# Standing rounded weights placed 64 bytes into longer ring buffers

## The chip, the cores and the metric

The kernel runs on one core of one Trainium2 chip. The metric is the device time of one execution in microseconds. Before the change three runs gave 2685.96, 2694.65 and 2699.78 us; the median is 2694.65.

## The reference

Two layers of a decoder trunk over 256 tokens of width 2048, all in float32. Each layer mixes the tokens by two groups of heads (attention with a window of 128, and RWKV-7 with a delta rule) and then runs a SwiGLU network; both are modulated by a condition vector. Cut to what matters here:

```python
mod = (cond @ w_ada[l] + b_ada[l]).reshape(B, 6, 1, D)      # cond = silu(c); w_ada 2048 x 12288
u = x * (1 + sc_m) + sh_m
proj = u @ w_in[l]                                          # 2048 x 4896
y = concat(sliding_window_attention(proj[..., :1536]), rwkv7_group(proj[..., 1536:]))
x = layer_norm(alpha * x + gt_m * (y @ w_out[l]))           # 2048 x 2048
u = x * (1 + sc_f) + sh_f
gate, up = split(u @ w_gate_up[l])                          # 2048 x 11264
x = layer_norm(alpha * x + gt_f * ((silu(gate) * up) @ w_down[l]))   # 5632 x 2048
```

## The kernel before

Every large product is computed from rounded parts. A float32 operand is split into hi, its value rounded to the type float32r, and lo, the rounded rest; the product is the sum of three matmuls, hi by hi, hi by lo and lo by hi. The activations are split once and kept in left-hand tiles (`lhsp`, 17 buffers of 2,048 bytes per partition, each with both parts of 128 rows by 256 tokens). The weights are split as they come. The helper `steps` (line 376) allocates a `raw` buffer of 1,024 columns from a ring of four, has SyncE's queue fill it from HBM, and lets ScalarE write `hi` (line 392, ring of three) and VectorE write `lo` as raw minus hi (line 393, ring of two). It yields slices of both, and two kinds of loops consume them:

- `stream` (line 402): the activation stands in the array as `lhsT`, and the weight streams as `rhs`, mostly in pieces of 512 columns. Lines 414, 415 and 417 are its three matmuls. It serves the q, k, v projection, the output projection, and both products of the SwiGLU network. Where `room` is given, `hi` and `lo` are other tiles than the rings'.
- `tstream` (line 420): the weight stands in the array, 128 columns of it at a time (32 in one block), and the 256 tokens of an activation stream. The result comes out transposed, features on partitions. Lines 426, 427 and 428 are its three matmuls: hi by hi, hi by lo, lo by hi. It serves the part of the input projection that feeds RWKV-7: in `front` (line 475) the low-rank columns, the values and, for the first layer, some of r and k; in `project` (line 588) the rest of r and k.

Every matmul of the program is a weight load and a matmul on TensorE; the profile has them as PEld and PE.

The work around it is ordered by hand. Within the mixer a written-out list per layer (`ORDER`, line 41) sets when projections, chunks of the recurrence, attention heads and output products come; a planner orders the instructions of each engine when the program is built, by dependences. SyncE's queue carries all large transfers; w_ada comes through it too, in tiles `ast` that VectorE multiplies into `aacc` (line 264) beside the other work, and in the first layer ahead of the projection (lines 302 to 319). That first stretch lasts until about 160 us.

On-chip memory is laid out pool behind pool: `const`, then `lhsp` (17 x 2,048 bytes), `wp` (raw 4, hi 3 and lo 2, each of 4,096 bytes), `adap` (two `asum` buffers of 32 bytes, `aacc`, two `ast`, two `arow` of 512 bytes), and behind them pools that are opened and closed stage by stage. At the largest stage 320 bytes per partition remain free. The start of `lhsp`, `wp` and of each buffer in them is a multiple of 128 bytes, and the slices taken are multiples of 512, so all rounded operands of the three matmuls begin at multiples of 128. `crow` (line 160) is the condition's row of 16 partitions by 128, used once at the start; `arow` (line 296) is a small row tile with two buffers, used where the gates are written out.

Of the kernel before, what the change touches and what calls it, by code (L numbers as in the profile page):

```python
# [10 lines left out]
F32 = mybir.dt.float32  # L11
F32R = mybir.dt.float32r
# [7 lines left out]
P = 128  # L20
# [3 lines left out]
KT = D // P  # L24
# [22 lines left out]
WB = (4, 3, 2)  # L47
# [14 lines left out]
SPLIT_F = (0, 8)  # L62
SPLIT_D = (1, 1)
TWO_PI = 2.0 * math.pi
IDLE = {"ada": 0, "first": 0, "dec": (0, 0), "ffn": (11, 6), "mix": 8}


@with_exitstack
def hybrid_trunk_kernel(
# [11 lines left out]
    const = ctx.enter_context(tc.tile_pool(name="const", bufs=1))  # L81
    lhsp = ctx.enter_context(tc.tile_pool(name="lhsp", bufs=17))
    wp = ctx.enter_context(tc.tile_pool(name="wp", bufs=2))
    adap = ctx.enter_context(tc.tile_pool(name="adap", bufs=1))
# [18 lines left out]
    def warm(b, n):  # L103

        for _ in range(n):
            PE.matmul(b[:, 0:T], lhsT=ident, rhs=rmask, start=True, stop=True)
# [50 lines left out]
    mods = [const.tile([P, 6 * KT], F32, name=f"mods{l}") for l in range(L)]  # L157
    nsink = [const.tile([P, 16], F32, name=f"nsink{l}") for l in range(L)]
    cond = const.tile([P, KT], F32, name="cond")
    crow = const.tile([KT, P], F32, name="crow")  # L160
    dma(crow, c.rearrange("b (j p) -> (b j) p", p=P))
    S.activation(crow, crow, AF.Silu)
    cb = bank()
# [56 lines left out]
    def rope(rp):  # L220
# [12 lines left out]
        magic = 1.5 * 2.0 ** 23  # L233
        V.tensor_scalar(kf, ang, 1.0 / TWO_PI, magic, ALU.mult, ALU.add)
        V.tensor_scalar_add(kf, kf, -magic)
        c1 = 6.28125
        c2 = float(np.float32(np.round((TWO_PI - c1) * 2 ** 20) / 2 ** 20))
        c3 = float(np.float32(TWO_PI - c1 - c2))
        for cc in (c1, c2, c3):
# [4 lines left out]
        wrap = rp.tile([P, 2, 32], F32, name="wrap")  # L244
        V.tensor_scalar(wrap, rc, math.pi, -TWO_PI, ALU.is_gt, ALU.mult)
        V.tensor_add(rc, rc, wrap)
# [28 lines left out]
    def ada_sums(l, mod, c0, blocks, idle=0):  # L275

        col = mod * KT + c0 // P
        n = len(blocks)
        sm = adap.tile([P, 8], F32, tag="asum", name="asum", bufs=2)
        for q in range(0, n, 4):  # L280
            b = bank()
            if q == 0:
                warm(b, idle)
            m = min(4, n - q)
            for i in range(m):
                PE.transpose(b[:, i * P:(i + 1) * P], blocks[q + i], ident)
            for i in range(m):
                bi = b[:, i * P:(i + 1) * P]
                if RED:
                    S.activation(bi, bi, AF.Copy, accum_out=sm[:, q + i:q + i + 1])  # L290
            if not RED:
                V.reduce_sum(sm[:, q:q + m], b[:, 0:m * P].rearrange("p (i k) -> p i k", k=P), axis=AX.X)
        V.scalar_tensor_tensor(mods[l][:, col:col + n], sm[:, 0:n], 1.0 if mod in (1, 4) else 0.0,
                               prm(l, "b_ada", col, n), ALU.add, ALU.add)
        if mod in (2, 5):
            row = adap.tile([8, P], F32, tag="arow", name="arow", bufs=2)[0:n]
            rb = bank()
            PE.transpose(rb[0:n, 0:P], mods[l][:, col:col + n], ident)
            S.copy(row, rb[0:n, 0:P])
            dma(gates[l, mod // 3, c0 // P:c0 // P + n], row)  # L300

    def ada_first(pool, c0, w):
# [14 lines left out]
        for m in range(2):  # L317
            ada_sums(0, m, c0, [acc[:, m, i * P:(i + 1) * P] for i in range(w // P)], IDLE["ada"] if m == 0 and c0 + w == D else 0)

# [20 lines left out]
    def pump():  # L340

        pace[1] += pace[0]
        while pace[1] >= 1.0:
            pace[1] -= 1.0
            next(ada_rest, None)
# [5 lines left out]
    def md(l, mod, kt, n=1):  # L351
        return mods[l][:, mod * KT + kt:mod * KT + kt + n]
# [20 lines left out]
                V.tensor_tensor(u[:, 1, :], uf, u[:, 0, :].bitcast(F32), ALU.subtract)  # L373
                us.append(u)

    def steps(srcs, W, kts, room=None):


        no = max(1, 1024 // W)
        for i0 in range(0, len(kts), no):  # L380
            m = min(no, len(kts) - i0)
            raw = wp.tile([P, 1024], F32, tag="raw", name="raw", bufs=WB[0])
            for dst, src in srcs(raw[:, 0:m * W].rearrange("p (k w) -> p k w", w=W), kts[i0], m):
                dma(dst, src)  # L384
            if room:
                parts = [(raw[:, o * W:(o + 1) * W], *room()) for o in range(m)]
            else:
                hi = wp.tile([P, 1024], F32R, tag="hi", name="hi", bufs=WB[1])
                lo = wp.tile([P, 1024], F32R, tag="lo", name="lo", bufs=WB[2])
                parts = [(raw[:, 0:m * W], hi[:, 0:m * W], lo[:, 0:m * W])]  # L390
            for fl, h, r in parts:
                S.copy(h, fl)  # L392
                ins = V.tensor_tensor(r, fl, h.bitcast(F32), ALU.subtract)  # L393
            anchor[:] = [ins.ins.name]
            for o in range(m):
                if room:
                    yield i0 + o, *parts[o][1:]
                else:
                    yield i0 + o, hi[:, o * W:(o + 1) * W], lo[:, o * W:(o + 1) * W]
            pump()  # L400
# [18 lines left out]

    def tstream(srcs, W, kts, us, blocks, first=True, last=True):  # L420

        for i, hi, lo in steps(srcs, W, kts):
            st, sp_ = first and i == 0, last and i == len(kts) - 1
            xh, xl = us[kts[i]][:, 0, :], us[kts[i]][:, 1, :]
            for c0, w, bt, opens, closes in blocks:
                PE.matmul(bt, lhsT=hi[:, c0:c0 + w], rhs=xh, start=st and opens, stop=False)  # L426
                PE.matmul(bt, lhsT=hi[:, c0:c0 + w], rhs=xl, start=False, stop=False)  # L427
                PE.matmul(bt, lhsT=lo[:, c0:c0 + w], rhs=xh, start=False, stop=sp_ and closes)  # L428
# [46 lines left out]
    def front(l, us, feeds, ahead=False):  # L475

        lb = [bank("lb", "cb") for _ in range(2)]
        vb = [acc_ps.tile([P, 512], F32, tag="acc", name="acc") for _ in range(4)]
        lblocks = [(0, 128, lb[0][:, 0:T], True, False), (128, 128, lb[0][:, T:2 * T], False, True),
                   (256, 32, lb[1][0:32, 0:T], not ahead, not ahead)]  # L480
        vblocks = [((2 * q + i) * P, P, vb[q][:, i * T:(i + 1) * T], i == 0, i == 1) for q in range(4) for i in range(2)]
        rk = None
        if ahead:
            b = ps.tile([P, 512], F32, tag="m1", name="rk0", bufs=1)
            turn[:] = 0, 0
            rk = [[b[:, 0:T], b[:, T:2 * T]], [lb[1][:, T:2 * T], None]]
            rblocks = [(0, P, rk[0][0], True, False), (P, P, rk[1][0], True, True), (2 * P, P, rk[0][1], False, True)]
            wrk = w_in[l][:, R0:R0 + 2 * RW].rearrange("(k p) (s n) -> p k s n", p=P, s=2)

            def rk_cols(rv, k0, m):  # L490
                return [(rv[:, :, 0:T], wrk[:, k0:k0 + m, 0, 0:T]), (rv[:, :, T:T + P], wrk[:, k0:k0 + m, 1, 0:P])]
        for kts, _ in feeds:
            fl = dict(first=kts[0] == 0, last=kts[-1] == KT - 1)
            if ahead and kts[0] == 0:
                tstream(rk_cols, T + P, kts, us, rblocks, **fl)
            tstream(cols(w_in[l], LORA0, 288), 288, kts, us, lblocks, **fl)
            if ahead and kts[0] > 0:
                tstream(rk_cols, T + P, kts, us, rblocks, **fl)
            tstream(cols(w_in[l], R0 + 2 * RW, RW), RW, kts, us, vblocks, **fl)
        return lb, vb, rk  # L500

    def mixer(l, us, mixp, feeds):
# [99 lines left out]
        def decays(g):  # L602
# [27 lines left out]
            if g == 0:  # L630
                warm(vt_, IDLE["dec"][l])
            for cc in range(NCH):
# [498 lines left out]
    def channel(l, ys, wa, fp):  # L1131
# [52 lines left out]
        us = []  # L1184
        parts = inputs(fp, z, l, "ln1_w", "ln1_b", l, 4, 3, us, SPLIT_F[l], IDLE["ffn"][l])

# [102 lines left out]
        us = []  # L1289
        feeds = front(l + 1, us, inputs(fp, z, l, "ln2_w", "ln2_b", l + 1, 1, 0, us, idle=IDLE["mix"]))  # L1290
        for t in range(2):
# [10 lines left out]
    with tc.tile_pool(name="pro", bufs=1) as pp:  # L1302
        xv = x[0].rearrange("(t p) d -> p t d", p=P)

        def parts():
            k0 = 0
            for n in PARTS:
# [13 lines left out]
                kts = list(range(k0, k0 + n))  # L1321
                make_u(pp, [xt[:, 0, :], xt[:, 1, :]], k0, lambda kt: md(0, 1, kt), lambda kt: md(0, 0, kt), us, kts, IDLE["first"] if k0 + n == KT else 0)
                k0 += n
# [44 lines left out]
```

## Time and profile before

| | |
|---|---|
| median of three runs | 2694.65 us (2685.96 to 2699.78) |
| profiled execution, its own time | 2691.27 us |
| its span, from the first to the last instruction | 2689.6 us |
| mean granted TensorE clock | 0.970 |
| instructions | 41844, of which 15375 matmuls |
| bytes moved | 637.50 MB, 237 GB/s in the mean |

The page's second part cuts the span into 40 slices of 67 us; each digit is a busy share in tenths, and PEclk is the clock that TensorE was granted.

```profile
PE   3789998789999999999999999989899999999997
DVE  6876767879877777777788676555754545545456
ACT  2364452445444444444445544444444444344442
PEclk9799997899999999999999999989999999999999
DMA  9968667598998888888878586434755655566654
```

A time window is a row of a table: the stretch in microseconds and its length, then for PE, PEld, DVE, ACT and POOL the busy time with the number of instructions in brackets, then the granted clock, the share of time the DMA engines were busy, and GB/s. Where such a table is for one line alone, it has the two columns PE and PEld. A row of the timeline is a start, a duration, the engine, the line, the operation with what it writes and reads, its shape, and how many were merged into the row; the duration of a merged row runs from the first start to the last end. A matmul's duration includes the time until its last result is out, and matmuls overlap, so the distance between starts is what one of them costs in a row of many.

### The profile page before, as it was taken

To read this page: it belongs to the slowest core of one execution; us is meant where nothing else is said; L and a number is where in the kernel's file an instruction comes from. 1 tells how busy PE (TensorE), PEld (TensorE's weight loads), DVE (VectorE), ACT (ScalarE), POOL (GpSimd) and SP (SyncE) were. 2 spreads that over 40 slices of the span, in tenths; PEclk is the share of its full clock that TensorE was granted. 3 is DMA by queue.
4 is the path that set the end of the run, shared out by engine and by line. 5 is a ranking of instruction groups with operands and counts; after the bars stand their busy time and mean duration, and the time that the engine had idled before them with its cause. 6 is when DMAs were issued, how large, how long until landed. Compare 5 with 4: busy or idle time off the path is not lost. (4 is left out here: it accounts for less than half of the span.)

```text
span 2689.6 us, 41844 instructions
## 1 busy us (share of the span) xinstructions
PE 2505.9 (93%) x15375; PEld 2097.0 (78%) x15375; DVE 1838.6 (68%) x2469; ACT 1187.4 (44%) x2029; POOL 132.5 (5%) x355
## 2 busy tenths in 40 slices
PE   3789998789999999999999999989899999999997
PEld 2787886567778888888889877867788888888887
DVE  6876767879877777777788676555754545545456
ACT  2364452445444444444445544444444444344442
POOL 1002112000000000000000022110000000000000
PEclk9799997899999999999999999989999999999999
DMA  9968667598998888888878586434755655566654
GB/s 312 382 200 254 194 194 236 174 330 293 348 331 300 301 304 311 292 300 308 299 270 304 178 258 182 109 83 160 237 173 187 193 183 196 196 191 189 192 188 149
DMA packets 352000, 637.50 MB, mean 237 GB/s; under 512 B 75894, under 2 KB 142898, under 8 KB 350258
## 3 DMA queue, kind: packets, MB, share of 16 engines
q1 hardware_dynamic: 351794, 634.82, 71.4%
q8 instruction: 121, 1.98, 0.3%
q14 instruction: 85, 0.70, 0.1%
HBM read 622.08 MB, written 12.62 MB: 236 GB/s over the span
## 5 line engine op out<-in xcount | busy, mean ns | idle before, releaser
L392 ACT CAST hi<-raw 128x1024 fp32r<-128x1024 f32 (+2 forms) x728 | 758.1, 1044 | 1104.5 <-PE acc L417 809.3
L393 DVE TENSOR_TENSOR lo<-raw,hi 128x1024 fp32r<-128x1024 f32 (+2 forms) x728 | 878.8, 1211 | 508.3 <-PE acc L415 340.6
L415 PE MATMUL acc<-lo,u 128*128 128x512 f32 x1568 | 514.1, 395 | 12.3 <-DVE lo L393 12.1
L417 PE MATMUL acc<-hi,u 128*128 128x512 f32 x1568 | 506.5, 391 | 0.0
L264 DVE SCALAR_TENSOR_TENSOR aacc<-ast,cond,aacc 128x1024 f32<-128x1024 f32 x300 | 383.8, 1279 | 140.4 <-DMA ast<-in_w_ada_dram 138.8
L414 PE MATMUL acc<-hi,u 128*128 128x512 f32 x1568 | 458.1, 394 | 0.8 <-ACT u L372 0.8
L415 PEld LDWEIGHTS acc<-lo,u 128*128 128x128 f32 x1568 | 293.8, 189 | 77.3 <-DVE lo L393 17.4
L414 PEld LDWEIGHTS acc<-hi,u 128*128 128x128 f32 x1568 | 295.3, 189 | 63.0 <-ACT u L372 1.0
L417 PEld LDWEIGHTS acc<-hi,u 128*128 128x128 f32 x1568 | 295.4, 188 | 62.0 <-issue 0.5
L415 PE MATMUL acc<-lo,ht 128*128 128x512 f32 (+1 forms) x720 | 243.6, 377 | 3.1 <-DVE lo L393 2.9
L417 PE MATMUL acc<-hi,ht 128*128 128x512 f32 (+1 forms) x720 | 242.2, 375 | 0.0
L426 PE MATMUL acc<-u,hi 128*128 128x256 f32 x720 | 206.2, 293 | 13.6 <-ACT hi L392 13.6
L414 PE MATMUL acc<-hi,ht 128*128 128x512 f32 (+1 forms) x720 | 217.0, 376 | 0.0
L427 PE MATMUL acc<-u,hi 128*128 128x256 f32 x720 | 204.6, 291 | 0.0
L428 PE MATMUL acc<-u,lo 128*128 128x256 f32 x720 | 193.2, 294 | 7.5 <-DVE lo L393 7.2
L415 PEld LDWEIGHTS acc<-lo,ht 128*128 128x128 f32 x720 | 135.1, 188 | 29.8 <-DVE lo L393 6.0
L426 PEld LDWEIGHTS acc<-u,hi 128*128 128x128 f32 x720 | 141.8, 197 | 18.3 <-ACT hi L392 14.5
L417 PEld LDWEIGHTS acc<-hi,ht 128*128 128x128 f32 x720 | 135.6, 188 | 24.3
L414 PEld LDWEIGHTS acc<-hi,ht 128*128 128x128 f32 x720 | 134.8, 188 | 24.3
L427 PEld LDWEIGHTS acc<-u,hi 128*128 128x128 f32 x720 | 141.8, 197 | 2.6 <-issue 1.6
L428 PEld LDWEIGHTS acc<-u,lo 128*128 128x128 f32 x720 | 133.7, 197 | 12.6 <-DVE lo L393 9.8
L1081 POOL TENSOR_TENSOR brs<-brs,mhalf 128x1 f32<-128x1 f32 x8 | 7.6, 955 | 1715.2 <-DVE brs L1080 774.6
(351 smaller groups left out, 2895.2 us busy)
## 6 DMA issues: line engine op xcount, KB each, us to landing
ast<-in_w_ada_dram SPq DMA_DIRECT2D x368, 512.0 KB
raw<-in_w_gate_up_dram SPq DMA_DIRECT2D x704, 256.0 KB
raw<-in_w_down_dram SPq DMA_DIRECT2D x176, 512.0 KB
raw<-in_w_in_dram SPq DMA_DIRECT2D x82, 512.0 KB
raw<-in_w_out_dram SPq DMA_DIRECT2D x64, 512.0 KB
raw<-in_w_in_dram SPq DMA_DIRECT2D x120, 256.0 KB
ast<-in_w_ada_dram SPq DMA_DIRECT2D x32, 256.0 KB
lnw<-in_ln_w_dram SPq DMA_DIRECT2D x4, 1024.0 KB
```

What stands on the lines that cost most here:

```text
L264: ins = V.scalar_tensor_tensor(acc, t, cond[:, j:j + 1], acc, ALU.mult, ALU.add)
L392: S.copy(h, fl)
L393: ins = V.tensor_tensor(r, fl, h.bitcast(F32), ALU.subtract)
L414: PE.matmul(bt, lhsT=xh, rhs=hi[:, c0:c0 + w], start=st, stop=False)
L415: PE.matmul(bt, lhsT=xh, rhs=lo[:, c0:c0 + w], start=False, stop=False)
L417: PE.matmul(banks[t][q][:, 0:w], lhsT=xl, rhs=hi[:, c0:c0 + w], start=False, stop=sp_)
L426: PE.matmul(bt, lhsT=hi[:, c0:c0 + w], rhs=xh, start=st and opens, stop=False)
L427: PE.matmul(bt, lhsT=hi[:, c0:c0 + w], rhs=xl, start=False, stop=False)
L428: PE.matmul(bt, lhsT=lo[:, c0:c0 + w], rhs=xh, start=False, stop=sp_ and closes)
L1081: G.tensor_tensor(rs[:, 0:1], rs[:, 0:1], mhalf[:, 0:1], ALU.pow)
```

## The change

The tiles `hi` and `lo` of the rings get 32 columns more (128 bytes, 4,224 instead of 4,096), and `steps` takes an offset into them. `tstream` asks for an offset of 16 columns, 64 bytes; `stream` for none. Both share the same rings, so a buffer is used now with the offset, now without. Five buffers of 128 bytes more are 640 bytes; `crow` moves from a place of its own in `const` into the ring of `arow`, which frees 512 bytes there.

```diff
+WOFF = 16
...
-    crow = const.tile([KT, P], F32, name="crow")
+    crow = adap.tile([KT, P], F32, tag="arow", name="crow", bufs=2)
...
-    def steps(srcs, W, kts, room=None):
+    def steps(srcs, W, kts, room=None, off=0):
...
-                hi = wp.tile([P, 1024], F32R, tag="hi", name="hi", bufs=WB[1])
-                lo = wp.tile([P, 1024], F32R, tag="lo", name="lo", bufs=WB[2])
+                hi = wp.tile([P, 1024 + 2 * WOFF], F32R, tag="hi", name="hi", bufs=WB[1])[:, off:off + 1024]
+                lo = wp.tile([P, 1024 + 2 * WOFF], F32R, tag="lo", name="lo", bufs=WB[2])[:, off:off + 1024]
...
     def tstream(srcs, W, kts, us, blocks, first=True, last=True):
 
-        for i, hi, lo in steps(srcs, W, kts):
+        for i, hi, lo in steps(srcs, W, kts, off=WOFF):
```

## The prediction

> **What bounds the kernel now.** I read the page's busy times first, then the time windows, then the timeline of TensorE inside them.
>
> ```profile
> span 2689.6 us, 41844 instructions
> PE 2505.9 (93%) x15375; PEld 2097.0 (78%) x15375; DVE 1838.6 (68%) x2469; ACT 1187.4 (44%) x2029; POOL 132.5 (5%) x355
> ```
>
> TensorE is busy 93% of the span, so time is won where the distance from one matmul to the next shrinks. The change touches the matmuls whose standing operand is a rounded weight: lines 426 to 428, one triple (one matmul each) per block. Five windows hold all of them. The first table is all work, the second the matmuls of line 426 alone; the count in brackets behind PE is what I need of it.
>
> ```profile
> 42.00:160.00 118.00, 90.47 (x612) 85.26 (x613) 95.56 (x134) 44.99 (x103) 0.00 (x0) 0.84 0.94 327
> 160.00:220.00 60.00, 55.92 (x510) 52.82 (x509) 44.22 (x71) 37.41 (x69) 1.27 (x5) 0.97 0.71 220
> 220.00:420.00 200.00, 189.74 (x1837) 159.37 (x1836) 142.05 (x213) 96.02 (x197) 40.69 (x101) 0.97 0.70 215
> 1395.00:1550.00 155.00, 147.93 (x1180) 137.17 (x1179) 120.02 (x185) 84.56 (x151) 2.26 (x7) 1.00 0.71 232
> 1550.00:1725.00 175.00, 161.54 (x1605) 136.02 (x1604) 114.33 (x171) 83.54 (x182) 43.88 (x101) 0.95 0.64 190
> ```
>
> ```profile
> 42.00:160.00 118.00, 55.92 (x188) 38.85 (x188) 0.84 0.94 327
> 160.00:220.00 60.00, 32.16 (x117) 22.36 (x117) 0.97 0.71 220
> 220.00:420.00 200.00, 36.95 (x128) 24.40 (x128) 0.97 0.70 215
> 1395.00:1550.00 155.00, 83.18 (x304) 56.31 (x304) 1.00 0.71 232
> 1550.00:1725.00 175.00, 37.74 (x128) 24.89 (x128) 0.95 0.64 190
> ```
>
> In 42 to 160 us the DMA engines are 94% busy and TensorE idles 27.5 of 118 us at a granted clock of 0.84: the transfers bound it, and a shorter matmul is worth nothing there. In the other four TensorE idles 4.1, 10.3, 7.1 and 13.5 us, 35 us of 590, while the DMA share is 0.64 to 0.71. They hold 117 + 128 + 304 + 128 = 677 triples, 2,031 matmuls. That these windows run at TensorE's pace is seen from the other side too, in the groups of 1395 to 1550 us:
>
> ```profile
> L393 DVE TENSOR_TENSOR lo<-raw,hi 128x1024 fp32r<-128x1024 f32 x35 | 42.6, 1218 | 14.5 <-PE acc L428 10.7 <-issue 1.8 <-PE lb L428 0.7
> L392 ACT CAST hi<-raw 128x1024 fp32r<-128x1024 f32 x36 | 37.8, 1049 | 30.5 <-PE acc L427 19.1 <-issue 3.5 <-DMA raw<-in_w_in_dram 3.1
> ```
>
> Both makers of the rounded weights wait mostly for TensorE to give a buffer back, 19.1 and 10.7 us, and only 3.1 us for a transfer.
>
> Now the matmuls themselves (start, duration, engine, line). First a steady stretch of standing weights, then one just behind four transposes:
>
> ```profile
> 1465.06 0.28 PE L426 MATMUL acc<-u,hi 128*128 128x256 f32 x1
> 1465.18 0.28 PE L427 MATMUL acc<-u,hi 128*128 128x256 f32 x1
> 1465.30 0.40 PE L428 MATMUL acc<-u,lo 128*128 128x256 f32 x2
> 1465.54 0.28 PE L426 MATMUL acc<-u,hi 128*128 128x256 f32 x1
> 1465.66 0.28 PE L427 MATMUL acc<-u,hi 128*128 128x256 f32 x1
> ```
>
> ```profile
> 1427.25 0.60 PE L366 MATMUL mb<-ident,z 128*128 128x128 f32 x4
> ...
> 1427.81 0.28 PE L426 MATMUL acc<-u,hi 128*128 128x256 f32 x1
> 1427.92 0.28 PE L427 MATMUL acc<-u,hi 128*128 128x256 f32 x1
> 1428.04 0.40 PE L428 MATMUL acc<-u,lo 128*128 128x256 f32 x2
> 1428.28 0.28 PE L426 MATMUL acc<-u,hi 128*128 128x256 f32 x1
> 1428.40 0.28 PE L427 MATMUL acc<-u,hi 128*128 128x256 f32 x1
> 1428.52 0.40 PE L428 MATMUL acc<-u,lo 128*128 128x256 f32 x2
> ```
>
> Steady: five steps in 0.60 us, 120 ns each. Behind the transposes: six steps from 1427.81 to 1428.52, 118 ns each, before it settles at 120. For a streaming weight (512 columns) the timeline has 15 steps from the first to the last of these rows:
>
> ```profile
> 399.77 0.39 PE L414 MATMUL acc<-hi,u 128*128 128x512 f32 x1
> ...
> 403.17 0.61 PE L414 MATMUL acc<-hi,u 128*128 128x512 f32 x2
> ```
>
> 3.40 / 15 = 226.7 ns. So 256 more columns cost 106.7 ns, a matmul of 256 columns has 106.7 ns of columns in its 120, one of 512 has 213.3 in its 226.7, and both carry the same 13.3 ns beside the columns. As 106.7 ns are 256 columns, 13.3 ns are 32 columns' time, or 128 bytes of a streamed row of four-byte numbers. That is what the change can touch: the standing weights now begin half of that length further on.
>
> **The change part by part.** *Standing weights 64 bytes into their buffers.* No instruction, byte or wait is added; only addresses move. Today every standing and streaming operand of these lines begins at the same place modulo 128 bytes: the 17 left-hand tiles are 2,048 bytes each and the ring buffers behind them 4,096, and all slices are multiples of 512. So no row here shows a rounded pair half a period apart, and the price of a step must be bounded. Three rows bound it from below and above.
>
> Lower end: the four transposes above take 0.60 us, and one alone 0.272 (median of the first row below), so (0.60 - 0.27) / 3 = 109 ns from one to the next, each with a weight load of 128 columns. A pair of load and matmul can follow the last one in that time, and 120 - 109 = 11 ns is the most there is to win per matmul.
>
> ```profile
> L366 PE MATMUL mb<-ident,z x80: 270/272/328, 638.1 to 1973.4; 128*128 128x128 f32 x80
> L1241 PE MATMUL mb<-ident,sg x176: 270/272/276, 699.9 to 2571.4; 128*128 128x128 f32 x176
> ...
> 2040.23 0.82 PE L1241 MATMUL mb<-ident,sg 128*128 128x128 f32 x6
> ```
>
> Upper end: the 13.3 ns are not a floor from above either. Behind an irregular start, streaming matmuls step at more than 226.7:
>
> ```profile
> 219.55 0.39 PE L417 MATMUL acc<-hi,u 128*128 128x512 f32 x1
> ...
> 220.94 0.39 PE L414 MATMUL acc<-hi,u 128*128 128x512 f32 x1
> ```
>
> Six steps in 1.39 us are 231.7 ns, 5 ns above the steady ones. So a pair out of step with its neighbour has cost from 2 ns less (118) to 5 ns more, and 11 less is the bound. What decides between the ends is whether the 13.3 ns hang on the address at all. For: they vary with how load and matmul meet (118, 120, plus 5), and steady stretches lock to exactly one period of 32 columns. Against: the transposes of z and of sg. By the sizes of the tiles ahead of them z begins 64 bytes past a multiple of 128 and sg on one, and both are loaded as the standing operand against the same identity; z steps at 109 ns, sg at (0.82 - 0.27) / 5 = 110. Half a period of the load's address changes nothing there. But those matmuls do not carry the 13 ns in either case, so they do not settle it. I take the value of the irregular stretch, 118, since it is the one row of this very form in which load and matmul meet otherwise than in the lock: 2 ns less.
>
> How much of a nanosecond arrives: in 160 to 220 and 1395 to 1550 us TensorE hardly waits, and I let all of it pass. In 220 to 420 and 1550 to 1725 us, with 256 of the 677 triples (38%), it already waits 10.3 and 13.5 us for other engines' chains, which a faster matmul does not shorten; I take it that four tenths are lost there, 15% of the whole. So 1 ns per matmul is 2,031 x 0.85 = 1.73 us. The 188 triples before 160 us count nothing; if that cover of transfers were gone they would add 188 x 3 x 1 ns = 0.56 us per nanosecond. The step is then -2 x 1.73 = -3.5 us. Its ends are -11 x 1.73 = -19 us (-28.5 with all 2,595 matmuls and nothing lost) and +5 x 1.73 = +8.7 us.
>
> [...]
>
> *The longer ring buffers.* Each is 4,224 bytes instead of 4,096, still a multiple of 128. But of the three hi buffers the middle one and of the two lo buffers one now lie 128 bytes off the multiple of 256 on which all of them stood. Streaming matmuls come in three kinds of equal count, two reading hi and one lo; the counts of the lo kind:
>
> ```profile
> L415 PE MATMUL acc<-lo,u 128*128 128x512 f32 x1568 | 514.1, 395 | 12.3 <-DVE lo L393 12.1
> L415 PE MATMUL acc<-lo,ht 128*128 128x512 f32 x624 | 216.9, 392 | 3.1 <-DVE lo L393 2.9
> L415 PE MATMUL acc<-lo,yl 128*128 128x512 f32 x224 | 81.2, 398 | 3.1 <-DVE lo L393 2.8
> ```
>
> That is 2,416, of which half meet the moved lo buffer, and 2 x 2,416 reads of hi, of which a third do: 1,208 + 1,611 = 2,819 matmuls. No row shows this offset; by the same steps as above the ends are -11 and +5 ns, -31 and +14 us. I take 0: the whole period of 128 bytes stays, and that is the only length at which the steady steps lock.
>
> *ScalarE's and VectorE's work on the moved tiles, the condition row in another pool.* The two makers write and read the same 1,024 elements per row, 1,049 and 1,218 ns each above, and in the windows they wait for TensorE; should they get longer, 19.1 and 10.7 us of waiting cover some 500 and 300 ns per tile there. The condition's row of 16 x 128 numbers now takes a turn in a ring of two whose next users come only after it has been read once near the start: no DMA, no activation and no queue position is added, 0. Everything behind the ring moves by 640 - 512 = 128 bytes: 0, by the same argument as for the ring.
>
> *Sum.* -3.5 us against the profiled execution's 2691.27 (span 2689.6 and 1.7 us around it) gives 2687.8. The median of the three runs is 2694.65, 3.4 us above that execution, and would give 2691.1. I say 2690.
>
> **The rivals.** *The excess goes altogether.* Half a period apart, load and stream stop meeting, and the step falls to 109: -19 us, 2672 from the execution and 2676 from the median; 2674. For it: the excess is exactly one period, as if the next matmul had to wait for its turn at the same place. Against: the irregular stretch wins only 2 of the 13 ns, and z against sg shows nothing.
>
> *Nothing changes* (the edit does not do what it says). The 13.3 ns belong to exchanging the weights, whatever their address: 2693. For it: they are the same at 256 and 512 columns. Against: they vary behind irregular starts.
>
> *Streaming pays.* The 2,819 matmuls that read a moved ring buffer step 5 ns later in the long stretches of lines 414 to 417, where nothing but TensorE counts: +14.1 us, 2705 from the execution, 2709 from the median; 2707. It decides from 13.5 / 2,819 = 4.8 ns on. For it: 5 ns is what a pair out of step costs at 219 us. Against: the lock is at 128 bytes, not 256.
>
> **How the numbers follow.** My forecast (steps of 113 to 119 ns) has 0.38, the excess gone 0.35, nothing changed 0.13, streaming pays 0.14. A difference counts as one from 0.5%, 13.5 us, about what a measurement of this kernel can tell from none. So faster is 0.35, the same 0.38 + 0.13 = 0.51, slower 0.14. The forecast's own range is 113 ns (-12 us) to no gain, 2680 to 2695. The wider range reaches from a little under the case of no excess, 2670, to streaming at its price, 2707; both signs together are why it is that wide.
>
> **What would show it.** In the timeline near 1465 us five steps of lines 426 to 428 take 0.57 to 0.60 us under my forecast, 0.55 if the excess is gone, 0.60 if nothing changes. The 15 steps of the streaming stretch stay at 3.40 us, or grow towards 3.45 or more where ring buffers pay. The busy time of line 426 in 1395 to 1550 us falls with the step, and the waits of the two makers for TensorE shrink. I am wrong if the steady step leaves 113 to 120, if streaming steps differ between ring buffers, or if steps shrink and the window does not, because a transfer or a vector chain takes the wait over.

## The result, and the profile after

The changed kernel takes 2706.26 us (median of 11 runs, 2698.19 to 2714.18) against 2692.26 for the kernel before (11 runs, 2683.29 to 2699.78): a ratio of 1.0058 [1.0045, 1.0071], 14 us more, slower by a little over the half per cent that counts here. The forecast was 2690; the time lies at the upper end of the range, where the rival "streaming pays" put it (2707).

First the head of the page of after, which answers to the first fence of the prediction. All lines have moved down by one: the triple of `stream` is now 415, 416, 418, that of `tstream` 427 to 429, and `hi` and `lo` are made in 393 and 394. (In the experiments below they lie up to six lines further; the engine and the operands tell them.)

```profile
span 2709.0 us, 41844 instructions
PE 2525.2 (93%) x15375; PEld 2092.6 (77%) x15375; DVE 1841.0 (68%) x2469; ACT 1186.6 (44%) x2029; POOL 133.9 (5%) x355
```

The instructions are the same, and so is their order on every engine but for three pairs of neighbours; TensorE is busy 19.3 us longer (2505.9 before), and the span is 19.4 us longer. The others keep their times within 2.4 us. So the time is in TensorE's own steps. The standing ones, in the timeline (start, duration, engine, line), near the place where the prediction read them:

```profile
1464.46 0.28 PE L427 MATMUL lb<-u,hi 128*128 128x256 f32 x1
1464.58 0.28 PE L428 MATMUL lb<-u,hi 128*128 128x256 f32 x1
1464.69 0.28 PE L429 MATMUL lb<-u,lo 128*128 128x256 f32 x1
1464.81 0.28 PE L427 MATMUL lb<-u,hi 128*128 128x256 f32 x1
1464.92 0.28 PE L428 MATMUL lb<-u,hi 128*128 128x256 f32 x1
1465.03 0.28 PE L429 MATMUL lb<-u,lo 128*128 128x256 f32 x1
```

Five steps in 0.57 us, 114 ns to the row's rounding, where there were 120; 113.3 by the exact starts. That is the low end of what the prediction gave its forecast (0.57 to 0.60). Now the streaming matmuls. The rows merge neighbours of one line; x2 is two of them.

```profile
1100.78 0.63 PE L416 MATMUL acc<-lo,u 128*128 128x512 f32 x2
1101.24 0.63 PE L418 MATMUL acc<-hi,u 128*128 128x512 f32 x2
1101.71 0.63 PE L416 MATMUL acc<-lo,u 128*128 128x512 f32 x2
1102.18 0.63 PE L418 MATMUL acc<-hi,u 128*128 128x512 f32 x2
1102.64 1.08 PE L415 MATMUL acc<-hi,u 128*128 128x512 f32 x4
1103.57 0.62 PE L416 MATMUL acc<-lo,u 128*128 128x512 f32 x2
1104.02 0.61 PE L418 MATMUL acc<-hi,u 128*128 128x512 f32 x2
1104.47 0.62 PE L416 MATMUL acc<-lo,u 128*128 128x512 f32 x2
1104.92 0.62 PE L418 MATMUL acc<-hi,u 128*128 128x512 f32 x2
1105.38 1.07 PE L415 MATMUL acc<-hi,u 128*128 128x512 f32 x4
1106.29 0.62 PE L416 MATMUL acc<-lo,u 128*128 128x512 f32 x2
```

From 1100.78 to 1102.64 are eight steps: 1.86 us, 232.5 ns each. From 1103.57 to 1105.38 are eight more of the same form: 1.81 us, 226.3 ns. Between them the ring goes from a pair of buffers that lies 128 bytes off the multiples of 256 to a pair that lies on them, as the sizes of the tiles ahead of them give; the `u` tile stands on a multiple of 256 throughout. The four steps from 1102.64 read the good buffer already and still take 230 ns each by the exact starts: here it takes a few matmuls to find the pace again. Before, a settled step was 226.7 everywhere.

Over the whole run I took the mean of the steps from the starts in the trace, standing ones under 160 ns and streaming ones under 300 ns, which leaves out waits and the stretches at a lower granted clock (2,200 to 2,300 standing, some 7,100 streaming of 512 columns):

| | standing, 256 columns | streaming, 512 columns |
|---|---|---|
| before | 119.5 ns | 227.3 ns |
| after | 114.9 ns | 230.6 ns |

7,100 x 3.3 ns = 23.4 us lost; 2,031 x 4.6 ns = 9.3 us in the stretches where the prediction counts it, for the gain. The makers of the weights point to the streaming lines too. The groups by line of before and of after (busy time and mean; idle time and what ended it):

```profile
L392 ACT CAST hi<-raw 128x1024 fp32r<-128x1024 f32 x706 | 741.2, 1052 | 1050.2 <-PE acc L417 809.3 <-PE acc L427 63.2 <-DMA raw<-in_w_gate_up_dram 47.0
```

```profile
L393 ACT CAST hi<-raw 128x1024 fp32r<-128x1024 f32 x706 | 740.1, 1051 | 1069.4 <-PE acc L418 849.0 <-PE acc L428 64.3 <-DMA raw<-in_w_gate_up_dram 48.9
```

ScalarE writes the rounded weights as fast as before, 1051 ns. Its idle time grows by 19.2 us, as the span does, and what of it the streaming line ended by 39.7 (809.3 to 849.0), more than the whole, so other waits shrink; what the standing line and the transfers ended hardly moves. Between the same instructions in both traces, the stretch that is 900 to 1390 us in before grows from 489.9 to 495.1 us, and that from 1930 us to the end from 745.6 to 756.2; both hold streaming matmuls and no standing weights.

One rival stands in the pages themselves: the mean granted clock is 0.970 in before and 0.965 in after. It does not make the main part of the loss. In those two stretches, which grow by 5.2 and 10.6 us, it is 1.00 and 0.99 in both profiles, and the kernel with the gap below takes a span of 2709.1 us at 0.971.

### The profile page after: what moved, and what is told of

It reads as the page before. It is cut to its first block, busy times and chain, and to the rows that moved or that the text cites. A ratio compares the mean times of both kernels' runs of the same rounds, so it can differ in the third digit from the quotient of the medians.

```text
span 2709.0 us, 41844 instructions
## 1 busy us (share of the span) xinstructions
PE 2525.2 (93%) x15375; PEld 2092.6 (77%) x15375; DVE 1841.0 (68%) x2469; ACT 1186.6 (44%) x2029; POOL 133.9 (5%) x355
## 5 line engine op out<-in xcount | busy, mean ns | idle before, releaser
L393 ACT CAST hi<-raw 128x1024 fp32r<-128x1024 f32 (+2 forms) x728 | 757.0, 1042 | 1123.9 <-PE acc L418 849.0
L427 PEld LDWEIGHTS acc<-u,hi 128*128 128x128 f32 x720 | 141.2, 196 | 23.3 <-ACT hi L393 19.2
```

## The experiments

The theory, called A in the expectations: a step depends on the streamed operand's address relative to that of the standing one that is loaded beside it, modulo 256 bytes. The 64 bytes of the standing weights gain, and the 128 bytes by which the longer buffers shift the streamed ones cost. The rivals: that the price comes with something else the change did (the offset itself, the alternation of offsets in one buffer, the condition's row, the tiles behind the ring), or that the address rule is one about single operands, not pairs.

**The ring alone.** The longer buffers and the moved row, no offset.

```diff
+                hi = wp.tile([P, 1024 + 2 * WOFF], F32R, ...)[:, off:off + 1024]   # lo alike
         for i, hi, lo in steps(srcs, W, kts):          # off stays 0
```

> The longer ring buffers alone: each hi and lo buffer is 4,224 bytes, the condition row stands in the other pool, and standing and streaming weights both lie at offset 0. Theory A (what the next matmul's place in the weights is against the streamed row, modulo 256 bytes, sets the step: in step at 0 it locks at 226.7 and 120 ns, at 128 it does not lock and takes about 232): streaming steps as irregular as in the changed kernel, mean 230 to 233 ns, standing steps back at 118 to 120, so slower than the changed kernel by its 10 us on standing weights and slower than before by 20 to 30 us, 2712 to 2722. Theory B (the alternating use of the buffers with and without the 64 bytes disturbs streaming, not their length): 226.7 and 120 ns, 2692 as before. Theory C (the 14 us come from waits and the order of the work around, not from the steps): 2692 as well.

2712.66 us (6 runs) against 2691.57: 1.0077 [1.0058, 1.0096], 21 us slower. The standing step is 119.0 ns, the streaming one 230.6, as in after. Its timeline shows a fast and a slow pace too:

```profile
1101.27 0.62 PE L416 MATMUL acc<-lo,u 128*128 128x512 f32 x2
...
1103.08 1.07 PE L415 MATMUL acc<-hi,u 128*128 128x512 f32 x4
1103.99 0.62 PE L416 MATMUL acc<-lo,u 128*128 128x512 f32 x2
...
1105.84 1.09 PE L415 MATMUL acc<-hi,u 128*128 128x512 f32 x4
```

Eight steps in 1.81 us, then eight in 1.85, 231 ns each; in the second stretch `lo` lies 128 bytes off and `hi` on a multiple of 256. The whole loss of the change, and more, is in the length of the buffers. 21 us of 7,100 x 3.3 = 23.4: some nine tenths of the steps' loss arrive in the time, with 16 to 26 us inside the interval.

**The standing offset alone.** Streaming weights are put back on multiples of 256 inside the longer buffers, and 128 bytes of padding put the tiles behind back too.

```diff
+    adap.tile([P, 32], F32, name="pad")
...
+                oh = off or (0, 0, 32)[slot[0] % 3]
+                ol = off or (32, 0)[slot[0] % 2]
```

> The standing weights' 64 bytes alone: rings of 4,224 bytes, but a streaming weight is put 128 bytes into those buffers that lie 128 off a multiple of 256, and 128 bytes are added behind the rings, so that every streamed and every left-hand operand of lines 414 to 417 is at 0 modulo 256 as before. Standing weights lie 64 bytes into their buffers, so at 64 or 192 modulo 256. Theory A: streaming steps 226.7 ns again, standing steps 113.3, about 7 ns on some 1,750 matmuls that count: -9 to -12 us from before, 2680 to 2683. Theory B: streaming stays irregular, 2706 as the changed kernel. Theory C: within 4 us of before.

2686.35 us (12 runs) against 2691.57: 0.9975 [0.9959, 0.9992]. Timeline, a standing stretch and a streaming one:

```profile
1464.56 0.28 PE L432 MATMUL acc<-u,hi 128*128 128x256 f32 x1
...
1465.46 0.28 PE L434 MATMUL acc<-u,lo 128*128 128x256 f32 x1
```

```profile
1100.10 0.62 PE L421 MATMUL acc<-lo,u 128*128 128x512 f32 x2
...
1104.63 0.62 PE L420 MATMUL acc<-hi,u 128*128 128x512 f32 x2
```

Eight standing steps in 0.90 us (113), and twenty streaming ones in 4.53 (226.5). The steps came as theory A expected them; of the 9 to 12 us expected from them, 5 came. Together the two halves give 21 - 5 = 16 us, where the change measured 14: within the intervals they add up, and nothing else in the change is needed.

**All weights at 64 bytes.** `stream` takes the offset as well.

```diff
-    def steps(srcs, W, kts, room=None, off=0):
+    def steps(srcs, W, kts, room=None, off=WOFF):
```

> Streaming weights also lie 64 bytes into the buffers, so at 64 or 192 modulo 256 against left-hand operands at 0 (tiles of lines 1245 at 128). Theory A with a lock at half a period as the standing weights show it: streaming steps fall by the same 6.7 ns to 220 ns, some 7,200 of them, -40 to -48 us, with the standing 113.3 about 2632 to 2645. If only an unchanged place from one matmul to the next locks, the change between 64 and 192 from buffer to buffer keeps streaming at 230 to 233 ns, 2706 as the changed kernel. Theory B (buffers used alike again, offset or not): 226.7 ns, 2681 to 2692.

2704.57 us (7 runs): 1.0048 [1.0026, 1.0071]. Streaming 230.8 ns in the mean, standing 114.9. So a streamed operand gains nothing at 64: theory A with its lock at half a period, 2632 to 2645 us, is refuted. Taken apart by the distance of streamed from standing operand, modulo 256, the mean streaming step is 227.0 ns at 0 (226.7 once settled) and 232.7 at 128 in the kernel with the gap below, where a distance lasts long; this one adds 229.3 at 64 and 232.7 at 192. Mixing offsets in a buffer isn't the cause: here none are mixed. That the change from buffer to buffer alone costs, the other branch of the expectation, falls with the gap and the sweep below, where the distance stays the same and the step is 232 to 233 all the same.

**A sweep by itself.** A kernel of its own that leaves the reference's computation out: rows of 48 matmuls, one offset each.

> None of the reference's work: only rows of 48 matmuls with a weight load each, rounded operands, nothing else running, 512 and 256 columns streamed from offset 0 while the standing operand lies 0, 16, 32, 48, 64, 80, 96, 112, 128, 160, 192 or 224 bytes on; then the other way round at 64, 128, 192. Theory A: 226.7 and 120 ns at 0; 220 and 113.3 at 64 and 192; 128 unlocked or slower, 230 to 233 and 118; offsets between lie on a line or at multiples of 16 bytes per 1.7 ns. If the place of the weights is nothing by itself: 226.7 and 120 everywhere.

It told nothing on the question. The rows of 512 columns (duration least, median, most; first and last start):

```profile
L35 PE MATMUL s512at0x<-mv,st x48: 1000/1153/1157, 48.8 to 87.4; 128*128 128x512 f32 x48
L35 PE MATMUL s512at64x<-mv,st x48: 1001/1153/1157, 206.5 to 245.0; 128*128 128x512 f32 x48
```

38.6 us over 47 steps are 821 ns each, whatever the offset, 3.6 times the step inside the large kernel, from the first row to the last (945 us in all). Why it ran at this pace stays open. Its windows print a granted clock of 1.00, but the trace of this run holds no record of the clock, so that figure is not shown. In the trace of before, steps of this form at a granted clock of 0.5 take 427 ns (median of 46), about half of 821.

**The sweep behind the kernel before.** The same, appended to the unchanged kernel behind its last store, with a first row of 160 that ends at the usual 227 ns a step: 64 matmuls a row, two alternating slices.

```diff
+        for o in range(0, 256, 16):
+            row(f"st{o}x", 256, 64, o, 0)      # standing operand o bytes on
+        for o in range(0, 256, 16):
+            row(f"mv{o}x", 512, 64, 0, o)      # streamed operand o bytes on
```

> The kernel before, and behind its last store rows of 64 matmuls with nothing else running: first 256 columns streamed from offset 0, while the standing operand lies 0, 16, ... 240 bytes past a multiple of 256; then 512 columns streamed from 0, 16, ... 240 bytes, with the standing operand at 0. Theory A in its simplest form (the next matmul waits for its turn within 128 bytes, so the excess is the rest of the period that the offset leaves): standing 120 ns at 0 and 128, 113.3 at 64 and 192, and on a line between, 116.7 and 110 at 32 and 96 or the other way round, not under the 109 of the transposes. A table of fixed levels instead (in step, half a step off): only 120 and 113.3. For streaming the runs with 64, 128 and 192 bytes of difference gave 229, 233 and 233 in their mixed stretches: by theory A these are settled levels and return here within 1.5 ns; if only the change from buffer to buffer costs, each row here settles at 226.7 or less. [...]

3107.03 us, the sweep included. Rows by tile, as above; a step is last minus first start over 63:

```profile
L1354 PE MATMUL st0x<-mv,sd x64: 277/283/283, 2745.0 to 2752.6; 128*128 128x256 f32 x64
L1354 PE MATMUL st64x<-mv,sd x64: 276/276/280, 2775.4 to 2782.5; 128*128 128x256 f32 x64
L1354 PE MATMUL st128x<-mv,sd x64: 274/281/287, 2805.4 to 2812.9; 128*128 128x256 f32 x64
...
L1354 PE MATMUL mv0x<-mv,sd x64: 389/389/398, 2866.1 to 2880.4; 128*128 128x512 f32 x64
L1354 PE MATMUL mv64x<-mv,sd x64: 388/392/397, 2925.3 to 2939.7; 128*128 128x512 f32 x64
L1354 PE MATMUL mv128x<-mv,sd x64: 390/393/404, 2984.5 to 2999.1; 128*128 128x512 f32 x64
L1354 PE MATMUL mv192x<-mv,sd x64: 388/393/398, 3044.2 to 3058.9; 128*128 128x512 f32 x64
...
L1354 PE MATMUL mv240x<-mv,sd x64: 387/388/396, 3089.0 to 3103.3; 128*128 128x512 f32 x64
```

With the exact starts, over a whole row: standing 119.9 ns at offset 0, 113.4 at 64, and 116.7 to 120.0 at the other fourteen; streaming 227.2 at 0, 229.1 at 64, 226.8 at 240, and 231.1 to 234.6 at the others. The medians in the rows show it too: 283 against 276, 389 against 392 and 393. So address alone does it, with nothing else running, and the kernel's three values (113, 227, 233) come back. But the theory in its simple form, a step that follows the distance by a line, falls: 64 is a single good place for the standing operand, 0 and 240 are good ones for the streamed one, and what lies between is neither a line nor two levels.

**A pitch of 256.** If the ring's length is the cause, buffers of 4,352 bytes (17 x 256) must take the loss away and leave the gain. `crow` and `arow` share one buffer to make room.

```diff
-                hi = wp.tile([P, 1024 + 2 * WOFF], ...)      # lo alike
+                hi = wp.tile([P, 1024 + 64], ...)
```

> Rings of 4,352 bytes per buffer, a whole number of 256, instead of 4,224; the 768 bytes that this takes come from the small row tile, which gets one buffer instead of two. Streaming weights all at 0, standing weights at 64 modulo 256 (but for some low-rank columns at 192). Theory A: streaming steps 226.7 ns as before, mean 227.3; standing steps 113.3 ns, mean 113.5 to 114.7; -7 to -11 us from before, 2681 to 2685, and 0 to 4 us better than with 64 and 192 mixed. If the gain of the run with 64 and 192 mixed was chance, 2692.

2688.80 us (12 runs) against 2692.81: 0.9988 [0.9976, 0.9999]; standing 114.8 ns, streaming 227.3. The loss is gone; of the gain, 4 us came where 7 to 11 were expected.

**A gap of 128 bytes in the kernel before.** Nothing but an unused tile between `lhsp` and `wp`. The rings move against `u` and `yl`, which lie ahead of the gap; `ht`, in a pool behind it, moves along. One run then holds the control beside the case.

```diff
+    gapp = ctx.enter_context(tc.tile_pool(name="gapp", bufs=1))
+    gapp.tile([P, 32], F32, name="gap")
```

> The kernel before with one unused gap of 128 bytes between the left-hand tiles and the weight buffers. Rings stay 4,096 bytes, no offset within a buffer, no change from buffer to buffer; every hi and lo is now 128 bytes off the tiles u and yl modulo 256, while the tiles ht behind the rings move with them and keep their place against hi and lo. Theory A: streaming against u and yl 231 to 233 ns, against ht 226.7 within the same run; standing weights 118 to 119; 5,400 x 5 ns: 20 to 28 us slower than before, 2712 to 2720. If it needs the change from buffer to buffer, 226.7 ns everywhere and 2692.

2710.11 us (4 runs) against 2692.81: 1.0072 [1.0047, 1.0096], 17 us for an empty tile. The mean streaming step is 231.2, so 7,100 x 3.9 = 27.7 us were there to lose, and 20 to 28 were expected: the share that arrives differs from kernel to kernel. Its timeline, against `u` and against `ht`:

```profile
1100.13 0.63 PE L417 MATMUL acc<-lo,u 128*128 128x512 f32 x2
...
1105.71 0.62 PE L417 MATMUL acc<-lo,u 128*128 128x512 f32 x2
```

```profile
1339.94 0.62 PE L419 MATMUL acc<-hi,ht 128*128 128x512 f32 x2
...
1343.57 0.61 PE L419 MATMUL acc<-hi,ht 128*128 128x512 f32 x2
```

24 steps in 5.58 us are 232.5 ns; 16 steps in 3.63 us are 226.9. The same weight buffers, at the same addresses, in the same run: slow against `u`, fast against `ht`. So it is the pair that counts, not the streamed operand's own place. What makes the 5.6 ns between the two stretches is not shown.

**Before once more**, for the spread from profile to profile.

> The kernel before, nothing changed but an unused constant: a second profile of it, to see how far two profiles of one kernel differ by themselves. In the profile shown of before the granted clock took 82.6 us of full speed, in the other kernels 93 to 98. If that is chance, this profile lies between 82 and 98; if the moved addresses cost clock, it stays at 80 to 85. Steps 226.7 and 120 ns by every theory.

2685.97 us, span 2684.3, 5.3 us less than the first profile of the same kernel. Its streaming step is 227.3 and its standing step 119.5, the same to a tenth. The steps repeat where the total doesn't; the stretches between equal instructions repeat within 2.6 us. The granted clock is 0.968, against 0.970 in the first profile; the other kernels have 0.964 to 0.972, and the gap, slow as it is, 0.971. Over their 12 runs the two kernels of the last pair below both have 0.968 in the mean. So it moves from profile to profile, and no effect of the addresses on it shows.

**A finer sweep**, in single elements of 4 bytes around the places of interest, built like the other.

> The kernel before with rows of 64 matmuls behind its last store, as in the earlier sweep, in steps of 4 bytes around the two places that settled: standing operand 0 to 12 and 48 to 76 bytes off with 256 columns streamed, streamed operand 228 to 252 and 0 to 12 bytes off with 512 columns. If the place within 16 bytes does not matter, the rows repeat the earlier ones in groups of four (113.4 for 64 to 76, 117.8 for 48 to 60; 227.2 for 0 to 12, 226.8 for 240 to 252, 233 for 228 to 236). If single elements count, some row leaves these by over 2 ns, up or down; one at 220 or 109 would be a better place than any tried.

2990.88 us with the sweep. Standing: 113.8 ns at 52, 113.3 at 64, 113.7 at 76, but 119.6 at 60 and 118.3 at 68. Streaming: 227.1 at 0, 236.7 at 4, 230.0 at 12, 239.3 at 244. And 240, 226.8 in the sweep before, is 236.5 here:

```profile
L1354 PE MATMUL mv0x<-mv,sd x64: 389/389/398, 2823.0 to 2837.3; 128*128 128x512 f32 x64
L1354 PE MATMUL mv4x<-mv,sd x64: 395/399/403, 2837.5 to 2852.4; 128*128 128x512 f32 x64
...
L1354 PE MATMUL mv240x<-mv,sd x64: 393/399/403, 2927.1 to 2942.0; 128*128 128x512 f32 x64
```

14.9 us for 63 steps at 240, where the row of the first sweep has 14.3, with other rows in front of it. So one offset can settle at more than one pace. The two sweeps also ran on different chips (0 and 64 came out alike on both); which of these makes the difference is not shown. Four bytes are enough to leave the good one. No place better than 0 for streaming or 64 for standing was found.

**The pitch of 256 without and with the 64 bytes**, on one chip, to price the offset alone. The two kernels differ in the one argument.

```diff
-        for i, hi, lo in steps(srcs, W, kts):
+        for i, hi, lo in steps(srcs, W, kts, off=WOFF):
```

> The rings of 4,352 bytes and the single small row buffer, with standing weights at 0 too: what the layout costs without any offset. Steps 226.7 and 120 ns, 2692 as before, within 0.2%. If the single row buffer or the longer rings cost something, 2694 to 2698, and the 64 bytes are worth that much more than the comparison with before showed.

> The rings of 4,352 bytes with standing weights at 64, again, on the same chip as the run without the offset: the 64 bytes alone. Standing steps fall by 4.75 ns in the mean, 2,592 of them, 12 us if all of it arrives: 0.4 to 0.5% under the run without the offset. If half is lost behind the transfers of the first 160 us and in waits, 0.15 to 0.3%.

Without: 2692.85 us (12 runs) against 2690.62, 1.0008 [0.9994, 1.0022]. With: 2687.52 (12 runs), 0.9983 [0.9970, 0.9996]. The windows of 1395 to 1550 us for line 427 alone, without and then with:

```profile
1395.00:1550.00 155.00, 83.60 (x304) 56.61 (x304) 0.99 0.71 232
```

```profile
1395.00:1550.00 155.00, 81.12 (x304) 55.36 (x304) 1.00 0.74 238
```

The same 304 matmuls are busy 2.5 us less. Buffers of 4,352 bytes, 17 x 256, as such cost nothing that these runs show, and the 64 bytes bring 5.3 us, 0.2%, or 3.1 against before. That version, like the padded one above, beats the changed kernel (2706) clearly, and the kernel before by less than the half per cent that counts here.

## Why the prediction was wrong, by its own steps

*What bounds the kernel: right.* TensorE's steps set the time: the span grew by TensorE's added busy time (19.4 and 19.3 us).

*The standing step: right in its sign, with two sizes wrong.* I took 118 ns, 2 less, from the one irregular stretch; it locks at 113.3 and is 114.9 in the mean, 4.6 less, between my value and my lower end of 11. The share that arrives was mis-sized the other way. 2,031 x 4.7 ns (119.5 to 114.8 at the pitch of 256) are 9.5 us, and 0.85 of it would be 8.1. Measured were 5.3 us (the last two kernels), 5.2 (the standing offset alone), 4.0 and 3.1 (the pitch of 256, twice, against before), each with an interval of several us. So the term of -3.5 us came out at -3 to -5: near by luck, a step too small times a share too large. Where the rest of the 9.5 us goes stays open. The spread of 2.6 us between equal stretches of two runs of one kernel is as large as what is sought in each, and the two makers' waits for the standing lines didn't shrink as I had written (63.2 and 64.3 us for ScalarE).

*The longer ring buffers: the step that failed.* "I take 0: the whole period of 128 bytes stays, and that is the only length at which the steady steps lock." At a distance of 128 a settled streaming step is 232.7 ns against 226.7, and with rings of 4,352 bytes, an odd multiple of 256, the mean is 227.3 as before: 256 is a period here, 128 is not. All ring buffers and all streamed operands stood on multiples of 256 before (only 99 loads of low-rank columns were 128 bytes off, mostly in runs too short to settle), so the trace of before could not show 128 as a period, and I inferred it from 13.3 ns being 32 columns' time. That number says how long the excess is; it does not say at which distances of addresses it stays. The step measured +21 us (the ring alone).

*Its upper bound: too low, in the count and in the price.* I counted the 2,819 matmuls that read a moved ring buffer and priced them at 5 ns, 14.1 us. A settled pair at 128 costs 6.0 ns (226.7 to 232.7), and by the addresses that the sizes of the tiles give, 3,424 streaming matmuls stand 128 bytes off their partner: 20.5 of the 23.4 us. "Everything behind the ring moves by 128 bytes: 0" was wrong for the same reason: `ht` lies behind the ring, so its pairs with the unmoved buffers went out of step, and only those with the moved ones kept their distance of 0. And a stretch that changes buffers loses its pace for some matmuls after each change, so that even where two neighbours both read unmoved buffers against `u` the step averages 228.9.

*z against sg.* Read as "against", it was of no weight in either direction, as the prediction itself said: those transposes, at 109 and 110 ns a step, do not carry the excess.

*The rivals and the numbers.* "Streaming pays" came true, in its place (the long stretches of `stream`) and with its sign. That its time meets the measured one (2707 against 2706.26) is luck: it put the streaming cost at 14 us where the ring alone cost 21, and left out the standing gain of 3 to 5 that gave part of it back. It had 0.14. "The excess goes altogether" and "nothing changes" fell, the second for both kinds of step. The warning sign was in the sum: the term taken as 0 touched more matmuls than the term it was added to, in stretches where TensorE alone counts, and its one row (231.7 ns behind an irregular start) was on the slow side.

## What to carry to other kernels

In this kernel of back-to-back rounded matmuls, the distance between the streamed operand and the standing one was a parameter of the time: 2.6% of a settled streaming step (226.7 to 232.7) and 5.5% of a standing one (119.9 to 113.3). When a buffer is made longer, keep its length a multiple of the pitch that the measured kernel had (256 here: with 4,224 bytes the ring alone cost 21 us, with 4,352 nothing that the runs show), and check what lies behind it; an empty 128-byte tile cost 17 us of 2690. In a prediction, count an unknown price by the number of instructions it multiplies before it is taken as 0.

## What the runs showed that was not expected

- Operands' addresses alone change a settled step: streaming 226.7 to 234.6 ns, and up to 239.3 in the fine sweep; standing 113.3 to 120.0, and 123.3 at 48 in the fine sweep.
- The grain is no coarser than 4 bytes (227.1 at 0, 236.7 at 4). The rows of the first sweep, 16 bytes apart, differ too: 226.8 to 234.6 for the streamed operand.
- A given offset has no single pace: 240 gave 226.8 and 236.5 for the streamed operand, 48 gave 117.8 and 123.3 for the standing one. No law of the distance was found, and why 52, 64 and 76 are good places for the standing operand is open.
- The sweep alone, outside the kernel, ran at 821 ns per 512 columns throughout, with no record of its clock; rows of the same form, appended to the kernel, ran at 227 to 239.
